# One-hots of the routing table on GpSimd, and the second layer's expert sums kept by token

## The chip, the cores and the metric

The kernel is one program on one core of a Trainium2 chip. The metric is device microseconds of one execution, and lower is better. The kernel before has a median of 5218.21 us over three runs (5210.64 to 5221.29).

## The reference

Two blocks of a model run one after the other on 256 tokens of 1024 channels. The first block has two layers. Each layer mixes tokens and then applies a mixture of 16384 small experts, `peer`; only that part is touched. In layer 0 it runs over 512 tokens (256 of the sequence and 256 of a context), in layer 1 over 256. Cut to what matters:

```python
def block(hc):
    q = (hc @ p['w_q']).reshape(chunk, PEER_HEADS, 2, PEER_HALF)
    s = jnp.einsum('thcd,hcnd->thcn', q, p['sub_keys'])
    s1, i1 = lax.top_k(s[:, :, 0], 16)
    s2, i2 = lax.top_k(s[:, :, 1], 16)
    ...                                   # top 16 of the 256 sums s1 + s2
    gw = jax.nn.softmax(best, axis=-1)
    u = jnp.take(p['peer_u'], eidx, axis=0)          # eidx = i1 * 128 + i2
    act = jax.nn.gelu(jnp.einsum('td,thkd->thk', hc, u)) * gw
    v = jnp.take(p['peer_v'], eidx, axis=0)
    return jnp.einsum('thk,thkd->td', act, v)
```

Each token so picks 128 pairs (i1, i2), 8 heads times 16, each with a weight gw.

## The kernel before, in words

Nothing is gathered. All 128 x 128 experts are computed densely, as 128 blocks e of 128 experts (e is i2's part of the index), and a **routing table** `wd[token, i1, e]` with the weights says what counts. `peer` has three parts.

**Route** (`peer_route`). After the query products, tokens go in blocks b of 128: four in layer 0, two in layer 1. For each block, VectorE finds the top 16 (`topk16`) and makes three arrays of 128 tokens by 128 picks: the two index parts and the weight. TensorE transposes them (`tps`), so that a pick lies on a partition and a token is a column; they land in `tr[0]`, `tr[1]` and `tr[2]`. ScalarE also writes the negatives of the first and the third into `tr[3]` and `tr[4]` (L1099).

**Table** (`peer_table`). For each token two 128x128 matrices are made: `qt`, the one-hot rows of the second index (VectorE, eight tokens in one instruction, L1112), and `pt`, the one-hot rows of the first index times the weight. Of every four tokens two `pt` are made by VectorE in one instruction (L1123), and two by ScalarE in two: the absolute difference from the index (L1120), then the positive part of weight minus weight times that (L1121). TensorE multiplies `pt` and `qt` (`wps`, two instructions for each token in the trace), ScalarE copies four tokens' results out of PSUM (`ws`, L1126), and each 32 tokens are stored by one DMA. A group g is 32 tokens; a block has four.

**Fills.** Expert work that needs no table is put beside the routing: `fill` computes `gelu(u.h)` of an expert block (`gelu_u`: a 512 KB load, a split into high and low parts by ScalarE, L238, and VectorE, L240, 24 products `s` on TensorE, L258, one Gelu) and stashes it in DRAM. 64 of the 128 expert blocks are stashed in each layer. In layer 0 sixteen of them stand behind the last table, in layer 1 four.

**Experts** (`peer_experts`). In groups of four expert blocks, the activations are multiplied with the table's columns, split into `ah` and `al`, the value rows are split into `vh` and `vl`, and `products` forms the three cross terms. In it the value rows are the stationary operand and the activations stream: 24 matmuls for each expert block, 512 columns each in layer 0 and 256 in layer 1. A PSUM tile takes the sum over the four blocks, and `done` (L1226) lets VectorE add it, times a modulation, into `x`. In layer 1 every other group has to compute its `s` first.

The order within an engine's queue is not the order of the code: a scheduler interleaves the instructions of all five engines by its own estimates and by which buffers come free. Each engine then runs its queue strictly in that order. So `s` products and `wps` products are mixed in TensorE's queue in a fixed way, and VectorE's `pt` and `qt` with the next block's top-16 work.

## Time and profile before

| | |
|---|---|
| median of three runs | 5218.21 us |
| the profiled execution | 5211.48 us, its span 5209.7 us |
| TensorE (PE) busy | 4967.9 us, 95% |
| VectorE (DVE) | 3488.0 us, 67% |
| ScalarE (ACT) | 2561.0 us, 49% |
| GpSimd (POOL) | 182.2 us, 3% |
| layer 0, tables of the four blocks | 1290.5 to 1697.3 us |
| layer 1, tables of the two blocks | 3831.7 to 4055.3 us |
| layer 1, experts | 4055.3 to 4626.1 us |

A TensorE matmul's end in the trace is modelled: one of 128 columns stands with 275 ns, while the next can start after less than half of that. So a high busy share hides waits, and the pitch of matmuls in a row (start to start) is what tells how long a piece of work needs. Records of one engine can overlap on VectorE and ScalarE too, by some tens of ns, so there also a pitch is shorter than a duration.

### The profile page before, as it was taken

How to read it: one execution, taken by the hardware profiler on the slowest of the kernel's cores; microseconds unless marked ns; L12 is line 12 of the kernel's file. 1: busy time of each engine (PE TensorE's matmuls, PEld its weight loads, DVE VectorE, ACT ScalarE, POOL GpSimd, SP SyncE). 2: the span in 40 equal slices, each digit the busy share in tenths (PEclk: the TensorE clock that was granted, in tenths of full speed). 3: DMA queues.
4: the chain of work that ended last, by engine and by line, in shares of the span. 5: the costliest groups of instructions: out<-in, count | busy, mean ns of one | idle time of the engine just before them, and what ended most of it. 6: DMA issues, size and time to landing. Idle time of an engine off the chain costs nothing.

```text
span 5209.7 us, 86462 instructions
## 1 busy us (share of the span) xinstructions
PE 4967.9 (95%) x33298; PEld 4170.8 (80%) x33298; DVE 3488.0 (67%) x7830; ACT 2561.0 (49%) x4754; POOL 182.2 (3%) x409
## 2 busy tenths in 40 slices
PE   8999998999999999999999999998899999989989
PEld 6677776678777888888887787877889999987888
DVE  4888878558995455555555566656796777765654
ACT  4345444534989322222223445445478544455564
POOL 0000001000000000000000010101000000000000
PEclk9999999999999999999999899888999999999999
DMA  4332323543444644444442332323656877733544
GB/s 137 107 91 88 90 81 93 167 151 101 160 171 163 234 144 142 142 143 142 143 146 70 111 84 78 85 61 92 210 187 222 279 227 238 226 116 118 167 131 146
DMA packets 432974, 740.50 MB, mean 142 GB/s; under 512 B 132210, under 2 KB 273202, under 8 KB 427826
## 3 DMA queue, kind: packets, MB, share of 16 engines
q1 hardware_dynamic: 431042, 732.29, 44.1%
q8 instruction: 262, 4.29, 0.3%
q10 hardware_dynamic: 1520, 2.69, 0.1%
q14 instruction: 150, 1.23, 0.1%
HBM read 622.37 MB, written 112.49 MB: 141 GB/s over the span
## 4 chain that ended last, share of the span: by engine, by line
PE 74%; ACT 12%; DVE 8%; DMA 3%; issue 2%; SPq 0%; ACTq 0%; POOL 0%; DVEq 0%; POOLq 0%
PE v L1180 20%; PE s L258 14%; PE zps L258 5%; ACT ws L1126 3%; PE adaps L279 3%; PE qps L258 2%; PE ops L258 2%; PE gtps L258 2%; ACT pt L1121 2%; PE ops L1368 2%; ACT whi L238 2%; ACT pt L1120 2%; PE bp L571 1%; DVE wlo L240 1%; PE zbps L258 1%
## 5 line engine op out<-in xcount | busy, mean ns | idle before, releaser
L258 PE MATMUL s<-h,whi 128*128 128x512 f32 (+1 forms) x4096 | 1058.7, 343 | 1.3 <-ACT whi L238 0.7
L240 DVE TENSOR_TENSOR wlo<-wraw,whi 128x1024 fp32r<-128x1024 f32 (+2 forms) x602 | 724.7, 1205 | 470.9 <-ACT whi L238 458.4
L238 ACT CAST whi<-wraw 128x1024 fp32r<-128x1024 f32 (+2 forms) x602 | 621.9, 1034 | 727.0 <-PE s L258 200.0
L258 PEld LDWEIGHTS s<-h,whi 128*128 128x128 f32 x4096 | 703.8, 191 | 68.6 <-ACT ge L1136 1.0
L258 PE MATMUL s<-h,wlo 128*128 128x512 f32 (+1 forms) x2048 | 704.2, 344 | 9.1 <-DVE wlo L240 9.1
L1180 PE MATMUL v<-al,vh 128*128 128x512 f32 (+1 forms) x2048 | 689.7, 337 | 0.6 <-DVE al L953 0.6
L1180 PE MATMUL v<-ah,vl 128*128 128x512 f32 (+1 forms) x2048 | 689.2, 337 | 0.0
L1180 PE MATMUL v<-ah,vh 128*128 128x512 f32 (+1 forms) x2048 | 682.7, 338 | 2.1 <-ACT ah L952 1.5
L952 ACT CAST vh<-vraw 128x1024 fp32r<-128x1024 f32 x256 | 261.9, 1050 | 719.2 <-PE v L1180 574.9
L1226 DVE SCALAR_TENSOR_TENSOR x<-v,mod,x 128x256 f32<-128x256 f32 x768 | 333.7, 477 | 272.6 <-PE v L1180 272.1
L1180 PEld LDWEIGHTS v<-ah,vh 128*128 128x128 f32 x2048 | 387.3, 190 | 49.7 <-ACT ah L952 9.4
L1180 PEld LDWEIGHTS v<-al,vh 128*128 128x128 f32 x2048 | 388.8, 190 | 46.3 <-DVE al L953 4.8
L258 PEld LDWEIGHTS s<-h,wlo 128*128 128x128 f32 x2048 | 390.3, 191 | 44.4 <-DVE wlo L240 10.3
L1180 PEld LDWEIGHTS v<-ah,vl 128*128 128x128 f32 x2048 | 388.1, 190 | 40.3 <-issue 1.4
L953 DVE TENSOR_TENSOR vl<-vraw,vh 128x1024 fp32r<-128x1024 f32 x256 | 308.6, 1220 | 98.9 <-ACT vh L952 98.9
L258 PE MATMUL zps<-h,whi 128*128 128x512 f32 (+3 forms) x896 | 293.6, 407 | 15.5 <-DVE lz L363 7.5
L1125 PEld LDWEIGHTS wps<-qt,pt 128*128 128x128 f32 x1536 | 215.8, 190 | 109.5 <-ACT pt L1121 91.2
L1125 PE MATMUL wps<-qt,pt 128*128 128x128 f32 x1536 | 272.3, 292 | 22.2 <-ACT pt L1121 13.6
L1126 ACT COPY ws<-wps 128x512 f32<-128x512 f32 x192 | 210.5, 1097 | 5.7 <-PE wps L1125 5.2
L258 PEld LDWEIGHTS zps<-h,whi 128*128 128x128 f32 (+1 forms) x896 | 167.5, 198 | 52.8 <-issue 16.6
L279 PE MATMUL adaps<-adaw,cs 128*2 128x128 f32 x1536 | 202.0, 274 | 5.4 <-DMA adaw<-ada 3.2
L1121 ACT ACTIVATE pt<-pt,tr,tr 128x128 f32<-128x128 f32 x384 | 180.4, 489 | 2.5
(614 smaller groups left out, 9617.4 us busy)
## 6 DMA issues: line engine op xcount, KB each, us to landing
wraw<-peu SPq DMA_DIRECT2D x256, 512.0 KB, 4.2
vraw<-pev SPq DMA_DIRECT2D x256, 512.0 KB, 4.5
wraw<-win SPq DMA_DIRECT2D x139, 512.0 KB, 3.6
adaw<-ada SPq DMA_DIRECT2D x96, 512.0 KB, 3.6
wd<-ws SPq DMA_DIRECT2D x24, 2048.0 KB, 6.8
wt<-wd SPq DMA_DIRECT2D x32, 1024.0 KB, 6.8
wraw<-w_q SPq DMA_DIRECT2D x32, 512.0 KB, 3.7
gd<-ge SPq DMA_DIRECT2D x64, 256.0 KB, 2.1
```

The costliest lines, as they stand in the source:

```text
L238: nc.scalar.copy(hi, raw)
L240: nc.vector.tensor_sub(lo, raw, hi.bitcast(F32))
L258: nc.tensor.matmul(out, w[wi][:, k, :], a[ai][:, k, ts], start=n == 0, stop=n == 3 * ko - 1)
L279: nc.tensor.matmul(ps[0:2, i * P:i * P + P], self.cs[:, k, :], w[:, k, :], start=k == 0, stop=k == KO - 1)
L952: self.nc.scalar.copy(hi, src)
L953: self.nc.vector.tensor_sub(lo, src, hi.bitcast(F32))
L1120: nc.scalar.activation(pt, self.iota, AF.Abs, bias=tr[3][:, cs])
L1121: nc.scalar.activation(pt, pt, AF.Relu, bias=tr[2][:, cs], scale=tr[4][:, cs])
L1125: nc.tensor.matmul(ps[:, t, :], pt, qt[:, t1 + t], start=True, stop=True)
L1126: nc.scalar.copy(ws[:, :, t0 + t1:t0 + t1 + 4].rearrange("p i t -> p t i"), ps)
L1180: nc.tensor.matmul(ps[:, m, :], va[i][wi][:, ms], aa[i][ai], start=n == 0, stop=n == 3 * GI - 1)
L1226: nc.vector.scalar_tensor_tensor(x[:, k, ts], src[:, m, ts], self.mod[l][:, 40 + k, s:s + 1], x[:, k, ts], op0=ALU.mult, op1=ALU.add)
```

## The change

Two parts. In the table, the two `pt` of every four tokens that ScalarE made are made by GpSimd, in the same single instruction that VectorE uses; `tr[3]` and `tr[4]` and what writes them go, and `pt` has six buffers in place of four. In layer 1 alone, the products swap operands: the activations of 128 tokens are stationary, and 512 channels of the value rows stream. Four PSUM tiles (two token halves, two channel halves) stay open over all 128 expert blocks. Nothing is added into `x` on the way; at the end `channels` copies the four sums out, transposes them in 16 pieces of 128x128, and calls `done` for each two.

```diff
@@ peer_route
-            tr = [rt.tile([P, T2], F32, name=f"tr{i}") for i in range(5)]
+            tr = [rt.tile([P, T2], F32, name=f"tr{i}") for i in range(3)]
...
                     nc.vector.tensor_copy(tr[n][:, b * P:b * P + P], ps[:, 0:P])
-                    if n != 1:
-                        nc.scalar.activation(tr[3 + n // 2][:, b * P:b * P + P], ps[:, 0:P], AF.Copy, scale=-1.0)
@@ peer_table
-                        pt = wb.tile([P, P], F32, tag="pt", name="pt", bufs=4)
-                        if t % 2:
-                            nc.scalar.activation(pt, self.iota, AF.Abs, bias=tr[3][:, cs])
-                            nc.scalar.activation(pt, pt, AF.Relu, bias=tr[2][:, cs], scale=tr[4][:, cs])
-                        else:
-                            nc.vector.tensor_scalar(pt, self.iota, tr[0][:, cs], tr[2][:, cs], op0=ALU.is_equal,
-                                                    op1=ALU.mult)
+                        pt = wb.tile([P, P], F32, tag="pt", name="pt", bufs=6)
+                        (nc.vector, nc.gpsimd)[t % 2].tensor_scalar(pt, self.iota, tr[0][:, cs], tr[2][:, cs],
+                                                                    op0=ALU.is_equal, op1=ALU.mult)
                         nc.tensor.matmul(ps[:, t, :], pt, qt[:, t1 + t], start=True, stop=True)
@@ peer_experts
+            def products_t(g, va, aa):
+                for i in range(GI):
+                    for b in range(2):
+                        bs = slice(b * P, b * P + P)
+                        for n, (wi, ai) in enumerate(((0, 0), (1, 0), (0, 1))):
+                            for c in range(2):
+                                nc.tensor.matmul(acc[b][c], aa[i][ai][:, bs], va[i][wi][:, c * 512:c * 512 + 512],
+                                                 start=g + i + n == 0, stop=g == P // GI - 1 and i == GI - 1 and n == 2)
+            def channels():
+                rows = []
+                for b in range(2):
+                    r = ep.tile([P, D], F32, tag="vraw", name="vrow", bufs=3)
+                    for c in range(2):
+                        (nc.scalar.copy, nc.vector.tensor_copy)[c](r[:, c * 512:c * 512 + 512], acc[b][c])
+                    rows.append(r)
+                for m0 in range(0, KO, 2):
+                    ps = ps_s.tile([P, 2, T], F32, tag="s", name="vt")
+                    for m in range(2):
+                        for b in range(2):
+                            nc.tensor.transpose(ps[:, m, b * P:b * P + P], rows[b][:, (m0 + m) * P:(m0 + m) * P + P],
+                                                self.ident)
+                    done(m0, ps, True)
+            if T == TX:
+                acc = [[ps_v.tile([P, 512], F32, tag="v", name="acc") for c in range(2)] for b in range(2)]
+                products = products_t
...
+            if T == TX:
+                channels()
```

The change also moves instructions. TensorE's queue in the second group of layer 0's first block, before (`s` is the fills' product, `wps` the table's):

```order
L1125 MATMUL wps<-qt,pt 128x128
L258 MATMUL s<-h_9713,whi 128x512
L258 MATMUL s<-h_9714,whi 128x512
L1125 MATMUL wps<-qt,pt 128x128 x2
L258 MATMUL s<-h_9713,wlo 128x512
L258 MATMUL s<-h_9713,whi 128x512
L1125 MATMUL wps<-qt,pt 128x128
L258 MATMUL s<-h_9714,whi 128x512
L1125 MATMUL wps<-qt,pt 128x128 x3
L258 MATMUL s<-h_9713,wlo 128x512
L258 MATMUL s<-h_9713,whi 128x512
L1125 MATMUL wps<-qt,pt 128x128
```

The same place now:

```order
L1119 MATMUL wps<-qt,pt 128x128 x10
L258 MATMUL s<-h_9713,whi 128x512
L258 MATMUL s<-h_9714,whi 128x512
L1119 MATMUL wps<-qt,pt 128x128 x6
L258 MATMUL s<-h_9713,wlo 128x512
L258 MATMUL s<-h_9713,whi 128x512
L1119 MATMUL wps<-qt,pt 128x128 x6
L258 MATMUL s<-h_9714,whi 128x512
L258 MATMUL s<-h_9713,wlo 128x512
L1119 MATMUL wps<-qt,pt 128x128 x10
L258 MATMUL s<-h_9713,whi 128x512
L258 MATMUL s<-h_9714,whi 128x512
```

The table's products stand close together, and of the fills' 24 products for an expert block two at a time stand between them; the rest follow behind the group. Counted over the whole queue, this is how many `s` products stand between the first table product of a group and that of the next, or, after a last group, up to the next block's table (up to the last table product, where no block follows):

| | before, groups 0, 1, 2, 3 | now |
|---|---|---|
| layer 0, block 0 | 44, 48, 58, 115 | 11, 38, 24, 192 |
| layer 0, block 1 | 40, 49, 48, 151 | 24, 48, 24, 192 |
| layer 0, block 2 | 42, 55, 64, 127 | 24, 48, 24, 192 |
| layer 0, block 3 | 41, 48, 49, 50 | 24, 48, 24, 6 |
| layer 1, block 0 | 102, 106, 116, 376 | 53, 143, 72, 432 |
| layer 1, block 1 | 92, 124, 101, 96 | 72, 144, 72, 10 |

VectorE's queue at the same group before (`qt` and `pt` are the table's, `best`, `pos`, `cand` and `tm` belong to the next block's top 16):

```order
L1112 TENSOR_TENSOR qt<-iota,tr_9788 128x1024
L1123 TENSOR_SCALAR pt<-iota,tr_9787,tr_9789 128x128 x2
L1013 MAX best<-tm 128x8
L1010 MAX best<-cand 128x8
L1014 MAX_INDEX pos<-best,tm 128x8
L1123 TENSOR_SCALAR pt<-iota,tr_9787,tr_9789 128x128 x2
L1112 TENSOR_TENSOR qt<-iota,tr_9788 128x1024
L1011 MAX_INDEX pos<-best,cand 128x8
L1123 TENSOR_SCALAR pt<-iota,tr_9787,tr_9789 128x128
L1012 MATCH_REPLACE tm<-best,cand 128x256
L1057 TENSOR_TENSOR cand<-v_11629 128x256
L1013 MAX best<-tm 128x8
```

And now:

```order
L1110 TENSOR_TENSOR qt<-iota,tr_9788 128x1024
L1117 TENSOR_SCALAR pt<-iota,tr_9787,tr_9789 128x128 x3
L1110 TENSOR_TENSOR qt<-iota,tr_9788 128x1024
L1117 TENSOR_SCALAR pt<-iota,tr_9787,tr_9789 128x128 x3
L1014 MAX_INDEX x_11562<-v_11561,tm 128x8
L1117 TENSOR_SCALAR pt<-iota,tr_9787,tr_9789 128x128
L1110 TENSOR_TENSOR qt<-iota,tr_9788 128x1024
L1117 TENSOR_SCALAR pt<-iota,tr_9787,tr_9789 128x128 x4
L1110 TENSOR_TENSOR qt<-iota,tr_9788 128x1024
L1117 TENSOR_SCALAR pt<-iota,tr_9787,tr_9789 128x128 x3
L1057 TENSOR_TENSOR cand<-v_11561 128x256
L1117 TENSOR_SCALAR pt<-iota,tr_9787,tr_9789 128x128 x2
```

The next block's top-16 work has moved out of the table's groups, most of it behind the fourth; VectorE's `pt` and `qt` follow each other nearly without a break. Counted in the same way, the first three groups hold 17, 53 and 36 instructions of top-16 work in layer 0's blocks 0, 1 and 2 (before 50, 76 and 36), and 27 in layer 1's block 0 (before 50).

TensorE's queue at the end of layer 1's experts, before (`v` is a product, `nps` the norm's sum, `pps` and `gps` belong to the next block of the model):

```order
L1180 MATMUL v<-ah,vh 128x256
L1180 MATMUL v<-al,vh 128x256
L1180 MATMUL v<-ah,vl 128x256
L324 MATMUL nps<-nsq,onesd 128x256 x4
L258 MATMUL pps<-hh_44421,whi 128x256 x2
L258 MATMUL gps<-hh_44421,whi 128x256
L258 MATMUL pps<-hh_44422,whi 128x256
```

And now (`acc` is the open sum, `vt` a transpose of the copied sum):

```order
L1186 MATMUL acc<-vh,ah 128x512 x2
L1186 MATMUL acc<-vl,ah 128x512 x2
L1186 MATMUL acc<-vh,al 128x512 x2
L1201 MATMUL vt<-ident,vrow 128x128 x12
L324 MATMUL nps<-nsq,onesd 128x256 x12
L1201 MATMUL vt<-ident,vrow 128x128 x4
L324 MATMUL nps<-nsq,onesd 128x256 x4
L258 MATMUL pps<-hh_42139,whi 128x256 x2
L258 MATMUL gps<-hh_42139,whi 128x256
```

Each stationary operand is used for two products in a row, and the norm's sums stand behind all products, no longer between them.

## Rows read from the trace of the kernel before

**Rows 1.** Busy time by routing block; its first line names the columns

```profile
core 0: us, PE busy (x) PEld busy (x) DVE busy (x) ACT busy (x) POOL busy (x), PEclk, DMA share, GB/s
1290.50:1392.60 102.10, 97.98 (x517) 74.19 (x516) 94.24 (x276) 93.36 (x187) 0.00 (x0) 1.00 0.45 165
1392.60:1500.40 107.80, 104.59 (x549) 80.94 (x548) 101.21 (x308) 95.15 (x190) 0.00 (x0) 1.00 0.46 166
1500.40:1597.00 96.60, 93.20 (x495) 70.49 (x494) 77.68 (x174) 91.55 (x184) 0.00 (x0) 1.00 0.41 150
1597.00:1697.30 100.30, 98.38 (x517) 73.86 (x516) 52.36 (x94) 88.15 (x183) 0.00 (x0) 1.00 0.46 168
3831.70:3955.30 123.60, 117.61 (x922) 110.61 (x923) 106.34 (x224) 111.73 (x221) 0.00 (x0) 1.00 0.61 216
3955.30:4055.30 100.00, 95.67 (x730) 87.84 (x729) 61.33 (x100) 97.05 (x200) 0.00 (x0) 1.00 0.58 201
```

**Rows 2.** Tile `pt`: count, ns min/median/max, first and last start

```profile
L1125 PE MATMUL wps<-qt,pt x1536: 270/275/378, 1292.3 to 4054.5; 128*128 128x128 f32 x192
L1120 ACT ACTIVATE pt<-iota,tr x384: 378/393/430, 1290.8 to 4052.2; 128x128 f32<-128x128 f32 x192
L1121 ACT ACTIVATE pt<-pt,tr,tr x384: 470/488/522, 1291.4 to 4053.7; 128x128 f32<-128x128 f32 x192
L1123 DVE TENSOR_SCALAR pt<-iota,tr,tr x384: 324/343/351, 1291.6 to 4051.9; 128x128 f32<-128x128 f32 x192
...
  ACT pt L1121: 104.8, 287
```

**Rows 3.** ScalarE by line, 1290 to 1700 us: busy us, mean ns

```profile
L1126 ACT COPY ws<-wps 128x512 f32<-128x512 f32 x128 | 139.8, 1092 | 5.2 <-PE wps L1125 5.2
```

**Rows 4.** VectorE by line, 1290 to 1700 us

```profile
L1112 DVE TENSOR_TENSOR qt<-iota,tr 128x1024 f32<-128x1024 f32 x64 | 78.0, 1218 | 2.3 <-PE wps L1125 2.1
```

**Rows 5.** GpSimd by line, whole span

```profile
L837 POOL TENSOR_TENSOR csum<-csum,lnc 128x256 f32<-128x256 f32 x7 | 5.2, 750 | 7.4 <-ACT lnc L836 6.7 <-ACT bs L578 0.7
...
masks.py:199 POOL TENSOR_SCALAR_AFFINE_SELECT ident<-ident 128x128 f32<-128x128 f32 x1 | 0.3, 292 | 0.1
```

**Rows 6.** Instructions of line 569, GpSimd copies of 128x128

```profile
L569 POOL COPY krp<-kr x224: 288/293/1266, 101.7 to 3621.8; 128x128 f32<-128x128 f32 x112
```

**Rows 7.** Timeline, three places of VectorE beside GpSimd: start us, us, instruction

```profile
884.30 1.26 POOL L837 TENSOR_TENSOR csum<-csum,lnc 128x512 f32<-128x512 f32 x1 [0.59 <-ACT lnc L836]
884.35 1.75 DVE L827 TENSOR_TENSOR lnc<-lnc,mean 128x512 f32<-128x512 f32 x1
...
3087.72 1.25 DVE L240 TENSOR_TENSOR wlo<-wraw,whi 128x1024 fp32r<-128x1024 f32 x1
3088.05 1.08 POOL L569 COPY krp<-kr 128x128 f32<-128x128 f32 x1 [0.15 <-PE bp L573]
...
4623.59 1.82 POOL L1472 MEMSET qe<- 128x2048 f32 x1
4623.81 1.63 DVE L1291 TENSOR_SCALAR bgh<-pv 128x32 f32<-128x32 f32 x1
```

**Rows 8.** Timeline, VectorE in the fourth table of layer 0

```profile
1643.29 1.22 DVE L1112 TENSOR_TENSOR qt<-iota,tr 128x1024 f32<-128x1024 f32 x1
...
1644.43 0.60 DVE L1123 TENSOR_SCALAR pt<-iota,tr,tr 128x128 f32<-128x128 f32 x2
```

**Rows 9.** Timeline, TensorE, eight table products in a row

```profile
1504.24 1.05 PE L1125 MATMUL wps<-qt,pt 128*128 128x128 f32 x8
```

**Rows 10.** Chain that ended last: start us, us, what

```profile
1856.49 21.76 PE s L258 x96
...
4179.43 23.04 PE v L1180 x192
...
4582.63 11.52 PE s L258 x96
```

**Rows 11.** Timeline, TensorE, the last sums of the norm in layer 1

```profile
4624.06 1.99 PE L324 MATMUL nps<-nsq,onesd 128*128 128x256 f32 x8 [1.08 <-ACT nsq L320]
```

## The prediction, made before the run

> **What bounds the kernel now.** I read the page's busy shares first (TensorE 95%), then the chain of waits, then the touched stages by stretch, then their instructions. The change touches two stages, and their limits differ.
>
> In layer 1's experts the chain is TensorE alone: 192 products take 23.04 us and the 96 `s` products of every other group 11.52 us [rows 10], so 0.120 us each, without a gap. ScalarE and VectorE feed it and are not waited for. What counts there is the pitch of products.
>
> In the tables TensorE looks 93 to 98% busy [rows 1], but that is modelled. A table product stands with 275 ns [rows 2], while eight in a row take 1.05 us [rows 9]: (1.05 - 0.275) / 7 = 0.111 us each. An `s` product of layer 0 takes 21.76 / 96 = 0.227 us [rows 10]. With the counts of `s` products from the queue's order and 256 table products for a block (28.4 us), the work in the six blocks is: layer 0, 265 x 0.227 + 28.4 = 88.5, then 93.7, 93.7 and 71.0 us; layer 1 (0.120), 112.4 and 78.0 us. Against the lengths in [rows 1] TensorE idles 13.6, 14.1, 2.9, 29.3, 11.2 and 22.0 us: 93 us in all, the most that the table's part can give beyond what a changed order hides.
>
> Who holds it up? ScalarE is busy 88 to 97% [rows 1], and its one-hots end most of the table's waits (104.8 us [rows 2]). But VectorE is as busy in layer 0's first two blocks (94.2 of 102.1, 101.2 of 107.8), because the next block's top 16 runs there. Only in the last blocks, 52.4 of 100.3 and 61.3 of 100.0, is ScalarE alone the limit.
>
> **The one-hots.** Removed from ScalarE: 384 x (0.393 + 0.488) = 338 us [rows 2]. For four tokens it keeps one copy of 1.09 us [rows 3] of about 2.85; it is no limit any more. Added on GpSimd: 384 instructions that the trace does not show. They depend on `tr` and on a free `pt` buffer, nothing else stands among them in GpSimd's queue, and behind each waits a table product, and behind that all of TensorE's queue.
>
> Their price, from both sides: at least 0.292 us (affine select, 128x128 [rows 5]; a copy of the size has 0.293 [rows 6]); a two-input add of 256 columns has 0.75 [rows 5], so 0.46 for 128 if I take 0.17 as fixed and halve the rest. I take 0.40, between them, since it reads one tensor and does two operations. Above this nothing in the trace bounds it; that risk is priced below. At 64 in a block even 0.46 is 29 us, so GpSimd by itself is no limit. The sign changes of L1099 go too; VectorE makes the first `qt` at that moment anyhow, so I count nothing for them, nor for the two more `pt` buffers.
>
> GpSimd and VectorE hinder each other, though. A VectorE add of 512 columns that began 0.05 us after a GpSimd add of 1.26 took 1.75 us, while one of 1024 columns takes 1.22 [rows 7, 4]. A GpSimd copy that usually takes 0.293 took 1.08 behind a VectorE subtraction [rows 7, 6]. And a VectorE `TENSOR_SCALAR` of 32 columns, the form that makes `pt`, took 1.63 and ended with GpSimd's memset [rows 7]. So all VectorE work of the table (`pt`, `qt`, the fills' `wlo`) excludes GpSimd's instruction, and the other way round. Only the start of the one that waits overlaps: the copy ended 0.16 us after the subtraction, 0.13 less than its 0.293. So one GpSimd one-hot delays VectorE by 0.40 - 0.13 = 0.27 us at most. I take 0.17, two collisions in three, and 0.125 where much single-input top-16 work lies between, with 0 and 0.46 as ends.
>
> [...]
>
> Now the blocks. VectorE's own pitch is 0.25 us for a `pt` and 1.14 for a `qt` [rows 8], so 64 x 0.25 + 16 x 1.14 = 34.2 us, plus four `wlo` (4.6) = 38.8 in a table of layer 0. A top-16 instruction costs 0.39 ((94.2 - 34.2 - 11.4) / 124). By the new order the first three groups hold 17, 53 and 36 of them: 45.4, 59.5, 52.8 and, in the last block, 38.8 us. With the delays (11, 8, 8, 11) the dense parts are 57, 67.5, 61 and, where TensorE's 102 x 0.227 + 28.4 = 51.5 is the longer, 54. The 192 `s` products behind the fourth group are 43.5 us of TensorE, which VectorE's remaining work (under 44) fits beside. The blocks become 100.5, 111, 104.5 and 54 + 19.5 (86 products that moved behind the table) = 73.5, against 102.1, 107.8, 96.6 and 100.3: -1.6, +3.2, +7.9, -26.8, together **-17 us**. Layer 1, with 12 and 14 `wlo`: 58.4 + 11 = 69.5 and, TensorE's 64.2 being the longer, 66; plus 432 and 115 products at 0.120, 51.8 and 13.8: 121.3 and 79.8 against 123.6 and 100.0: **-22 us**.
>
> **The sums by token.** Columns stay the same, instructions halve: 3072 x 0.120 = 368.6 us become 1536 at layer 0's pitch for 128x512, 0.227 [rows 10] = 348.2: -20.4. At 0.120 for 256 columns and 0.227 for 512 each instruction carries some 0.013 us, and half of those go. VectorE loses 31 x 8 additions, which were hidden. Bounds: 0 if a shared bank or a late operand eats it, -21 at best; I take the row's pitch. The end: before, from 4594.15 (the last `s` piece's end [rows 10]) to 4626.05 (the norm's end [rows 11]) is 31.9 us. Now 96 x 0.227 = 21.8, two copies on each of two engines (1.2, by the 1.09 of [rows 3] for a strided one and less for these), the first transposes and additions (1.2), 16 squares on ScalarE at about 0.4 (6.4) and the last sums (0.5): 31.1. So the end pays itself but not the 1.3 us that its last products saved: **-20 us**.
>
> **The sum.** -17 - 22 - 20 = -59 us. From the profiled execution's 5211.5: 5152; the median of the runs shown is 6.7 above that one, so 5152 to 5159. I say **5156 us**.
>
> **Rivals.**
> *The port decides, slower.* Each one-hot delays VectorE by its whole 0.46 us and no start overlaps. For: the 1.63 us row; all of VectorE's table work contends, and the new order packs it densely. Against: the handovers in the same rows do overlap. The blocks change by +16, +25, +29, -13, +16 and -7, +66 in all; with -20, 5258 us. The point from which it decides: above 0.22 us of delay, where TensorE's work no longer covers the last blocks, the six blocks change by -110 + 384 x the delay, so with the -20 the whole is even at 0.34 us. The same if GpSimd by itself needs 1.1 us from start to start.
> *The port costs nothing.* Then the blocks give -13, -5, 0, -29, -11 and -22, and with -20 the time is 5112 us. For: TensorE's queue has 24 `s` products in each group as slack. Against: rows 7.
> *Only the sums pay.* The new order takes the `s` products from the tables, VectorE is the limit in layer 0's first blocks anyhow, and what the last blocks win the others lose: 5211.5 - 20 = 5191 us.
>
> **Chances.** My forecast (20 to 85 us won) 0.50; free port 0.13; only the sums, or a net within 10 us of nothing, 0.14, of which two fifths count as faster; the port or a slow GpSimd instruction 0.23. About 0.2%, 10 us, is what a measurement can tell from no change. Faster by more 0.69, within 0.09, slower 0.22. The range goes from the free port's 5112 to just short of the first rival's 5258: 5110 to 5250. The likeliest case's own range is 5127 to 5191.
>
> **What would show it.** GpSimd's 384 one-hots at 0.3 to 0.5 us, and VectorE's `pt` above 0.343 and `qt` above 1.22 in the mean, by what they wait. Layer 0's last block at 70 to 78 us and layer 1's at 76 to 84; the first three of layer 0 within 10 us of before. The products at a 0.227 pitch, 33.3 us for two groups instead of 34.56. Wrong would be: a one-hot above 0.6 us, blocks of layer 0 above 120 us, or a pitch of products above 0.235.

## The result: slower by 1.0%, and the profile after

The changed kernel takes 5268.59 us (median of 4 runs, 5256.34 to 5286.2) against 5214.86 for the kernel before on the same chip: a ratio of 1.0104, 95% interval [1.0081, 1.0126]. Forecast were 5156 us, with 5110 to 5250 as the range. Of the profiled executions the changed one took 5256.34 us (span 5254.5), 44.8 more in the span than the one before.

First the stretches, cut at the same places as in [rows 1]; the first line names the columns. Lines 1 to 4 are the routing blocks of layer 0, the fifth the fills that are left behind the fourth, the next two the blocks of layer 1.

```profile
core 0: us, PE busy (x) PEld busy (x) DVE busy (x) ACT busy (x) POOL busy (x), PEclk, DMA share, GB/s
1284.90:1400.60 115.70, 99.05 (x520) 80.89 (x519) 95.91 (x262) 53.74 (x57) 68.98 (x64) 1.00 0.41 147
1400.60:1522.00 121.40, 105.64 (x547) 86.68 (x546) 104.40 (x316) 55.04 (x59) 72.22 (x64) 0.99 0.41 147
1522.00:1646.50 124.50, 107.14 (x542) 88.51 (x541) 85.38 (x186) 54.20 (x58) 74.47 (x64) 0.96 0.40 144
1646.50:1728.00 81.50, 66.96 (x382) 55.00 (x381) 47.94 (x87) 40.36 (x43) 70.94 (x64) 1.00 0.38 136
1728.00:1819.20 91.20, 91.20 (x404) 75.50 (x403) 31.93 (x32) 33.13 (x43) 0.00 (x0) 1.00 0.81 282
...
3863.50:4003.80 140.30, 122.39 (x909) 115.37 (x910) 108.38 (x225) 72.56 (x89) 74.53 (x64) 0.95 0.56 195
4003.80:4102.00 98.20, 82.91 (x625) 76.75 (x624) 59.73 (x97) 52.11 (x64) 72.57 (x64) 0.98 0.49 177
```

TensorE's share falls from 95 to 98% to 82 to 87%: it waits more than before, and that although ScalarE, 88 to 97% busy in [rows 1], is down to about half. GpSimd, which did nothing here, is busy 69 to 75 us in each block with 64 instructions, so 1.08 to 1.16 us for each. Layer 0's tables with the fills behind them take 534.3 us, 55.8 more than the same stretch of before; layer 1's tables 238.5 against 223.6.

What the instructions of the tile `pt` take in the changed kernel (ns min/median/max), and below it who ended the waits (us, times):

```profile
L1117 POOL TENSOR_SCALAR pt<-iota,tr,tr x384: 785/792/4097, 1285.2 to 4100.6; 128x128 f32<-128x128 f32 x192
L1117 DVE TENSOR_SCALAR pt<-iota,tr,tr x384: 326/358/553, 1286.0 to 4099.4; 128x128 f32<-128x128 f32 x192
...
  POOL pt L1117: 224.1, 288
```

An undisturbed one-hot on GpSimd takes 0.785 us; VectorE makes the same tile in 0.34 [rows 2]. The waits that ScalarE's one-hots ended (104.8 us, [rows 2]) are gone, and GpSimd's end 224.1 us instead. Both figures add the waits of TensorE's products and of their weight loads, so one standstill can count twice. The products alone, first before and then now, waited for

```profile
  ACT pt L1121: 13.6, 54
...
  POOL pt L1117: 90.8, 95
```

so 77 us more, while the tables' stretches above grew by 55.8 and 14.9 us, the latter although 13.8 us of products have left it. The chain of waits over the first 35 us of the first table says the same, share by line and its first pieces (start us, us, what):

```profile
by line: POOL pt L1117 83.1%; PE wps L1119 12.1%; DMA gd<-ge 6.6%; PE s L258 1.3%; issue 0.6%
...
1285.19 7.79 POOL pt L1117 x6
1292.98 0.04 issue
1293.03 0.73 PE wps L1119 x4
1293.75 12.11 POOL pt L1117 x11
```

And the timeline there, VectorE, GpSimd and the table products:

```profile
1291.09 1.22 DVE L1110 TENSOR_TENSOR qt<-iota,tr 128x1024 f32<-128x1024 f32 x1
1291.09 8.25 POOL L1117 TENSOR_SCALAR pt<-iota,tr,tr 128x128 f32<-128x128 f32 x7
...
1293.03 1.26 PE L1119 MATMUL wps<-qt,pt 128*128 128x128 f32 x6 [1.15 <-POOL pt L1117]
1293.78 0.47 DVE L1117 TENSOR_SCALAR pt<-iota,tr,tr 128x128 f32<-128x128 f32 x1 [0.73 <-PE wps L1119]
...
1297.85 0.49 PE L1119 MATMUL wps<-qt,pt 128*128 128x128 f32 x2 [0.94 <-POOL pt L1117]
```

`qt` keeps its 1.22 us. GpSimd's seven one-hots run without a gap and still take 8.25 us, 1.18 each. VectorE waits for a buffer that TensorE has not yet freed, TensorE for GpSimd.

The second layer's sums did what was forecast of them. The chain that answers to [rows 10]:

```profile
4158.64 11.51 PE s L258 x96
4170.15 21.79 PE acc L1186 x96
```

96 products of 512 columns take 21.79 us, 0.227 each; two groups take 33.30 instead of 34.56 us. From the last table's end to the end of the norm it is 567.0 us instead of 570.75, with 115 more `s` products (13.8 us) in it: 17.6 us won.

One more difference is not the change's. The mixer of layer 1, which the change does not touch, is 20.8 us shorter; its line in the kernel before, and in the changed one:

```profile
2835.10:3690.00 854.90, 801.24 (x7618) 667.73 (x7619) 547.54 (x1462) 412.69 (x919) 82.42 (x194) 0.88 0.32 93
```

```profile
2885.90:3720.00 834.10, 780.62 (x7607) 652.48 (x7608) 545.26 (x1460) 413.03 (x918) 85.92 (x194) 0.90 0.33 95
```

TensorE was granted 0.90 instead of 0.88 of its clock there; the 10 us with the lowest grant have 0.50 in both kernels. That is chance as far as these traces tell: from the mixer's first product to its last the changed kernel takes 859.8 us at 0.90, and the run with the one-hots alone, which has the same instructions there, 872.2 us at 0.89. The medians, 53.7 us apart, show more of the change's cost than the two profiles do.

### The profile page after: what moved, and what is told of

The parts are those of the page before. It is cut to its first block, busy times and chain, and to the rows that moved or that the text cites. A ratio compares the mean times of both kernels' runs of the same rounds, so it can differ in the third digit from the quotient of the medians.

```text
span 5254.5 us, 82985 instructions
## 1 busy us (share of the span) xinstructions
PE 4938.7 (94%) x31778; PEld 4110.7 (78%) x31778; DVE 3414.6 (65%) x7584; ACT 2331.1 (44%) x3976; POOL 618.7 (12%) x793
## 4 chain that ended last, share of the span: by engine, by line
PE 76%; DVE 9%; POOL 6%; ACT 5%; DMA 2%; issue 2%; SPq 0%; ACTq 0%; DVEq 0%; POOLq 0%
PE s L258 17%; PE v L1174 13%; PE acc L1186 7%; POOL pt L1117 6%; PE zps L258 4%; PE adaps L279 3%; PE qps L258 2%; PE ops L258 2%; PE gtps L258 2%; PE ops L1393 2%; DVE wlo L240 1%; PE yp L557 1%; PE bp L571 1%; PE zbps L258 1%; PE up L580 1%
## 5 line engine op out<-in xcount | busy, mean ns | idle before, releaser
L258 PE MATMUL s<-h,whi 128*128 128x512 f32 (+1 forms) x4096 | 1023.0, 340 | 3.2 <-ACT whi L238 2.6
L1117 POOL TENSOR_SCALAR pt<-iota,tr,tr 128x128 f32<-128x128 f32 x384 | 433.7, 1144 | 751.6 <-DVE tr L1097 371.8
L1174 PE MATMUL v<-ah,vl 128*128 128x512 f32 x1024 | 401.6, 392 | 0.0
L1174 PE MATMUL v<-al,vh 128*128 128x512 f32 x1024 | 400.2, 391 | 0.0
L1174 PE MATMUL v<-ah,vh 128*128 128x512 f32 x1024 | 393.3, 391 | 0.5
L1251 DVE SCALAR_TENSOR_TENSOR x<-v,mod,x 128x256 f32<-128x256 f32 x512 | 220.1, 478 | 209.4 <-PE v L1174 209.4
L1119 PE MATMUL wps<-qt,pt 128*128 128x128 f32 x1536 | 256.1, 298 | 97.5 <-POOL pt L1117 90.8
L1174 PEld LDWEIGHTS v<-ah,vh 128*128 128x128 f32 x1024 | 190.9, 188 | 47.6 <-ACT ah L952 7.3
L1174 PEld LDWEIGHTS v<-al,vh 128*128 128x128 f32 x1024 | 192.3, 188 | 45.3 <-DVE al L953 3.9
L1174 PEld LDWEIGHTS v<-ah,vl 128*128 128x128 f32 x1024 | 192.2, 188 | 40.8 <-issue 1.4
L1117 DVE TENSOR_SCALAR pt<-iota,tr,tr 128x128 f32<-128x128 f32 x384 | 139.8, 387 | 123.9 <-PE wps L1119 120.9
```

What stands on the lines that cost most here:

```text
L258: nc.tensor.matmul(out, w[wi][:, k, :], a[ai][:, k, ts], start=n == 0, stop=n == 3 * ko - 1)
L1117: (nc.vector, nc.gpsimd)[t % 2].tensor_scalar(pt, self.iota, tr[0][:, cs], tr[2][:, cs], op0=ALU.is_equal, op1=ALU.mult)
L1119: nc.tensor.matmul(ps[:, t, :], pt, qt[:, t1 + t], start=True, stop=True)
L1174: nc.tensor.matmul(ps[:, m, :], va[i][wi][:, ms], aa[i][ai], start=n == 0, stop=n == 3 * GI - 1)
L1251: nc.vector.scalar_tensor_tensor(x[:, k, ts], src[:, m, ts], self.mod[l][:, 40 + k, s:s + 1], x[:, k, ts], op0=ALU.mult, op1=ALU.add)
```

## The experiments

Three theories stood at the start. **Rate:** GpSimd's one-hot is simply dearer than the prediction's highest price (0.785 us against 0.46), and TensorE waits for it. **Port**, by the prediction's name for it (the traces show who waits, not a port): what hurts is that VectorE and GpSimd exclude each other, so that VectorE too loses time. **Buffers:** with 6 buffers for `pt`, GpSimd can't run ahead and begins too late. Each experiment's ratio is to the kernel before on its chip. "Dense part" is the time from a block's first `qt` to the end of its last `ws` copy, read from the traces. Moving one-hots to another engine, or giving them more buffers, also lets the scheduler change the order within the queues; where that bears on a reading it is said.

| dense parts, us | L0 1st | 2nd | 3rd | 4th | L1 1st | 2nd |
|---|---|---|---|---|---|---|
| changed kernel | 77.6 | 83.5 | 86.8 | 82.6 | 98.9 | 99.3 |
| a quarter on GpSimd | 68.4 | 74.9 | 66.5 | 70.5 | 94.0 | 89.8 |
| all on VectorE | 55.8 | 61.5 | 55.8 | 55.7 | 73.8 | 74.0 |
| all on VectorE, GpSimd beside for nobody | 57.3 | 63.1 | 57.7 | 57.3 | 76.4 | 75.9 |
| changed, 16 buffers | 75.5 | 77.6 | 82.4 | 78.4 | 91.1 | 91.0 |
| a quarter on GpSimd, 16 buffers | 51.3 | 60.1 | 48.3 | 51.4 | 69.3 | 77.2 |
| changed, cheap operation | 55.8 | 65.3 | 62.3 | 63.8 | 72.1 | 78.7 |

### The sums alone

The routing lines are those of before; of the diff only `products_t` and `channels` stay.

> The second part of the change alone: ScalarE makes half of the one-hots as before, the second layer's expert sums are the new ones. In the trace of the changed kernel the stretch of layer 1's experts is 3.7 us shorter although 115 s products (13.8 us) moved into it, so 17.6 us are won there. Theory 1 (GpSimd's one-hot is twice as dear as predicted and nothing else failed): the sums pay 17 to 20 us, so 5195 to 5199 against 5215, and the blocks of the tables stay as before within 3 us each. Rival (the shorter sums only paid because the s products came later): under 8 us won, 5207 or more.

Measured: 5195.57 us against 5210.31, ratio 0.9965 [0.9949, 0.998]. That is 14.7 us, with 10 to 27 in the interval; in the profiles the final norm's `fr` starts 19.4 us earlier, 2.0 of which were won ahead of the last table, so 17.4 in the experts. The rival (shorter only because work came later) falls: here nothing was moved, and it is as much.

### The one-hots alone

```diff
-            if T == TX:
+            if False:
                 acc = [[ps_v.tile(...)
...
-            if T == TX:
+            if False:
                 channels()
```

> The first part alone: one-hots on VectorE and GpSimd in turn, sums by channels as before. If the two parts add up, this is the changed kernel's 5268.6 plus the 17.6 us of the sums, 5286; with the clock's share in the mixer (20.8 us shorter in the changed kernel's profile, by a higher granted clock) taken as chance, up to 5290. Theory 1 and the port rival agree here. Should it come out under 5260, the two parts hinder each other and the sums carry part of the loss.

Measured: 5298.16 us against 5210.31, ratio 1.016 [1.0138, 1.0182]; 8 us more than the highest figure expected. Its dense parts are those of the changed kernel within 1 us but for layer 1's first (101.3). So the whole loss sits in the one-hots, 72 to 95 us of it, and the sums give a part of it back.

### A quarter on GpSimd

```diff
-(nc.vector, nc.gpsimd)[t % 2].tensor_scalar(pt, ...
+(nc.vector, nc.vector, nc.vector, nc.gpsimd)[t].tensor_scalar(pt, ...
```

> The changed kernel, but GpSimd makes only the fourth of each four one-hots, VectorE the other three. 32 on GpSimd in a block at the 1.08 us from start to start that the changed kernel shows are 35 us, under TensorE's 51 to 64; VectorE's dense part becomes 96 x 0.25 + 16 x 1.14 + 4.6 = 46.8 us plus top 16. Theory 1 (GpSimd's rate is the limit, 64 x 1.08 = 69 us in a block): the limit goes, blocks of layer 0 near 97, 111, 104 and 65 us, layer 1's near 121 and 85: 5170 to 5190. Rival, the port (VectorE is held up by each of GpSimd's instructions): half of the hindrance stays and VectorE has more to do, the blocks stay above 105, 118, 115 and 72: 5215 to 5240.

Measured: 5224.34 us against 5210.31, ratio 1.0022 [1.0007, 1.0038]. The port theory's figure, not the rate's: with half of the work GpSimd still ends 183.8 us of waits. One place in the timeline, which repeats every 3.7 us, shows why:

```profile
1291.67 1.22 DVE L1110 TENSOR_TENSOR qt<-iota,tr 128x1024 f32<-128x1024 f32 x1
1291.69 2.80 POOL L1117 TENSOR_SCALAR pt<-iota,tr,tr 128x128 f32<-128x128 f32 x2 [1.18 <-PE wps L1119]
...
1293.70 0.49 PE L1119 MATMUL wps<-qt,pt 128*128 128x128 f32 x2 [0.99 <-POOL pt L1117]
1294.22 1.09 ACT L1120 COPY ws<-wps 128x512 f32<-128x512 f32 x1 [1.09 <-PE wps L1119]
1294.23 0.35 DVE L1117 TENSOR_SCALAR pt<-iota,tr,tr 128x128 f32<-128x128 f32 x1 [0.31 <-PE wps L1119]
```

GpSimd idles 1.18 us for a buffer, begins when `qt` begins, and two one-hots take 2.80 us; TensorE waits 0.99 for the first. `qt` keeps its 1.22 us. So neither theory as stated: GpSimd had time enough on average, but started at the worst moment.

### All on VectorE

```diff
-(nc.vector, nc.gpsimd)[t % 2].tensor_scalar(pt, ...
+(nc.vector, nc.vector)[t % 2].tensor_scalar(pt, ...
```

> The changed kernel, but VectorE makes all the one-hots and GpSimd none. VectorE's dense part is 128 x 0.25 + 16 x 1.14 + 4.6 = 54.8 us plus top 16 (7 to 21 us) in layer 0, about 66 us in layer 1. Theory 1: VectorE is the limit, a little shorter than GpSimd's 69 us: blocks of layer 0 near 105, 119, 112 and 67, layer 1's near 130 and 92: 5210 to 5230. Rival, the port: with GpSimd silent VectorE also loses the hindrance, pt 0.358 to 0.343 us and no gaps, and the time falls below that of the kernel with a quarter on GpSimd.

Measured: 5160.04 us against 5210.31, ratio 0.9893 [0.9874, 0.9911]. VectorE's dense part was estimated at 54.8 us plus top 16, and layer 0's first measures 55.8. The top 16 does not fit beside it: the new order has moved it out. Between a block's first `qt` and its last one-hot VectorE's work other than `qt`, `pt` and `wlo` takes 0.7, 7.0 and 1.1 us in layer 0's first three blocks, in the changed kernel 12.0, 23.4 and 20.1. The time lies 50 us below the 5210 expected at least. The port theory had foretold the order of this one and the quarter on GpSimd; the next run tells whether for its reason.

### GpSimd's work beside it, waited for by nobody

To the kernel with all one-hots on VectorE this adds, at the start of each block's table:

```diff
+        for n in range(64):
+            cs = slice(b * P + 2 * n + 1, b * P + 2 * n + 2)
+            gh = wb.tile([P, P], F32, tag="gh", name="gh", bufs=2)
+            nc.gpsimd.tensor_scalar(gh, self.iota, tr[0][:, cs], tr[2][:, cs], op0=ALU.is_equal, op1=ALU.mult)
         for g in range(b * 4, b * 4 + 4):
```

> All one-hots that anything uses come from VectorE; GpSimd makes 64 more of them in each block into tiles that nobody reads, so no instruction waits for GpSimd. Theory 1 (GpSimd's rate is what hurts: someone waits for its results): no change against the kernel with all one-hots on VectorE, 5150 to 5170, the tables' dense parts stay at 55.8, 61.5, 55.8, 55.7, 73.8 and 74.0 us. The port theory: each of GpSimd's instructions takes its 0.785 us from VectorE, 64 x 0.785 = 50 us in a block, less what falls on VectorE's idle time: dense parts 90 to 106 us in layer 0 and up to 120 in layer 1, the time 5300 to 5440 though nobody waits for the work added. A third, half of the hindrance: dense parts near 80 us, about 5260.

Measured: 5163.91 us against 5211.13, ratio 0.9923 [0.9895, 0.9952]. The kernel without the added work had 0.9893: 64 one-hots beside VectorE in each block cost the whole kernel 0.3%, within what the intervals leave open. The dense parts grow by 1.5 to 2.6 us, so 0.02 to 0.04 us for each. The two engines in this kernel:

```profile
L1108 POOL TENSOR_SCALAR gh<-iota,tr,tr x384: 782/864/3908, 1294.5 to 4023.4; 128x128 f32<-128x128 f32 x192
...
L1121 DVE TENSOR_SCALAR pt<-iota,tr,tr x768: 322/388/476, 1295.4 to 4012.1; 128x128 f32<-128x128 f32 x192
```

GpSimd's 64 are busy 72.8 us in the first block, so 1.14 each, with nothing in their way but VectorE. The port theory falls: the two do interfere, but it is GpSimd that pays.

### Prices

In front of the kernel before stands a list of instructions; the timed lines, in short:

```diff
+ 274  8 x gpsimd.tensor_scalar(128 columns, is_equal, mult, two numbers per partition)
+ 276  8 x the same, is_equal alone
+ 278  8 x is_equal, mult with fixed numbers      280  8 x add, mult with fixed numbers
+ 282  8 x as 274, 512 columns
+ 287 24 x vector.tensor_tensor(1024 columns, add)    289 16 x gpsimd as 274
+ 293 48 x vector.tensor_scalar(128 columns)          295 16 x gpsimd as 274
```

> The kernel before with a list of instructions in front: GpSimd's one-hot of 128 columns eight times with VectorE idle, the same with one operation, with immediate numbers, with add and multiply, with 512 columns; then 16 of them beside 24 VectorE additions of 1024 columns, and 16 beside 48 VectorE one-hots. After the run in which GpSimd's work lay beside VectorE's without harm the theories are: A, GpSimd alone waits, and only behind two-input VectorE work: 0.79 us alone and beside VectorE's one-hots, near 1.1 + 0.79 from start to start beside the additions, VectorE's pitch unchanged (1.14 and 0.25) in both. B, both wait for each other in any form: VectorE's one-hots at 0.25 + 0.79 for each GpSimd instruction between. For the price itself: if 512 columns take four times 128 the price is by column (3.1 us), if under 1.5 us it is mostly fixed.

The timeline of GpSimd and VectorE (start us, us, instruction); line 276 overlaps the end of the additions and is left out:

```profile
2.75 9.93 POOL L274 TENSOR_SCALAR bo<-bsrc,bsc 128x128 f32<-128x128 f32 x8 [1.44 <-DVE bsc L267]
...
20.08 4.89 POOL L278 TENSOR_SCALAR bo<-bsrc 128x128 f32<-128x128 f32 x8
24.94 2.12 POOL L280 TENSOR_SCALAR bo<-bsrc 128x128 f32<-128x128 f32 x8
27.05 16.44 POOL L282 TENSOR_SCALAR bo<-bsrc,bsc 128x512 f32<-128x512 f32 x8
...
43.95 23.21 POOL L289 TENSOR_SCALAR bo<-bsrc,bsc 128x128 f32<-128x128 f32 x16
...
67.61 15.30 POOL L295 TENSOR_SCALAR bo<-bsrc,bsc 128x128 f32<-128x128 f32 x16
```

```profile
3.73 13.60 DVE L287 TENSOR_TENSOR bv<-bw 128x1024 f32<-128x1024 f32 x10
...
68.00 7.31 DVE L293 TENSOR_SCALAR bv<-bw,bsc 128x128 f32<-128x128 f32 x26
```

Alone a one-hot takes 0.787 us (the last ones of line 295, after VectorE stopped; the first of line 274 has 0.805). 512 columns take 2.05, so (2.05 - 0.787) / 384 = 3.3 ns a column and some 0.37 us besides. Fixed numbers make it 0.61, and an addition in place of the comparison 0.265 from start to start: it is the comparison that is dear. Beside VectorE's one-hots it is 0.83 (eight of line 295), and VectorE's stand at 7.31 / 26 = 0.28 instead of 0.25 [rows 8]. Beside two-input additions without a gap each takes 1.40 (line 274 from the third on), one for each addition, and here VectorE loses too: 1.39 us from start to start instead of 1.14 [rows 8] (the 13.60 us above also hold three additions beside line 276). In the second stretch the additions took turns with VectorE's one-hots, and GpSimd's took 1.50 each. So theory A is right that the form of VectorE's work decides and that GpSimd waits most, though its 1.9 us beside the additions was too much. Its "VectorE's pitch unchanged" fails: a two-input instruction loses 0.25 us, far from the 0.79 of theory B.

### Sixteen buffers

```diff
-name="pt", bufs=6)
+name="pt", bufs=16)
```

> The changed kernel with 16 buffers for one-hots instead of 6, so that GpSimd can run further ahead while TensorE works through a row of s products. Theory 3 (six buffers leave GpSimd idle in those rows): layer 1's dense parts fall from 98.9 and 99.3 to 80 to 85 us, layer 0's from 77 to 87 to 70 or so, the time to 5200 to 5230. Port theory (VectorE and GpSimd take turns: a group of 32 tokens costs 16 x 0.25 + 4 x 1.14 + 1.15 + 16 x 0.785 = 22.3 us, whoever waits): dense parts within 5 us, 5250 to 5270.

Measured: 5233.39 us against 5211.13, ratio 1.0049 [1.0032, 1.0067]; by the ratios 0.55% or 29 us less than the changed kernel. Between the two theories: the dense parts fall by 2 to 8 us, most in layer 1, where the rows of `s` products are longest. Against the kernel before the loss falls from 1.04 to 0.49%, so by about half; the rest stays. GpSimd's 64 one-hots of a block all lie in its dense part: with 6 buffers they are busy 70 to 75 us of it and GpSimd idles 8 to 26 us, with 16 they are busy 72 to 79 us and it idles 4 to 15.

### A quarter on GpSimd, and none, with sixteen buffers

The edit of the quarter above and 16 buffers; and the edit of all on VectorE and 16 buffers.

> VectorE three one-hots of four, GpSimd the fourth, with 16 buffers instead of 6. With 6 buffers the trace shows GpSimd beginning its one-hot at the moment a qt begins, waiting its 1.2 us, and TensorE waiting for that one-hot, 18 us for 32 tokens. Theory 3 (too few buffers let GpSimd begin only then): with 16 the wait is hidden, a group costs VectorE's 24 x 0.27 + 4 x 1.14 + 1.15 = 12.2 us or GpSimd's 8 x 0.79 + 4 x 1.1 = 10.7, dense parts of layer 0 50 to 56 us against 66 to 75, the time 5140 to 5165. Rival (GpSimd at such a rate holds the table up in any case): dense parts above 62, 5185 or more.

> All one-hots on VectorE, 16 buffers. VectorE waited only 5 us for TensorE in these instructions with 6 buffers, so both theories expect no change: 5150 to 5165. It is the yardstick for the quarter on GpSimd with 16 buffers: if that one is 10 us or more faster than this, GpSimd's help pays; if this is the faster, any work on GpSimd costs more than VectorE's own.

Measured: 5128.48 us against 5214.5, ratio 0.9842 [0.9823, 0.9861], for the quarter; 5155.57, ratio 0.9888 [0.9872, 0.9904], for none. The quarter beats both kernels and all others that leave nothing out. It is 12 us under the range that theory 3 gave, and GpSimd's help pays: 27 us against none. With 6 buffers the quarter was at 5224: ten more buffers are worth 1.8% here. They also let the scheduler move work: between the first `qt` and the last one-hot of the six blocks stand 12.2 us less of VectorE's other work than with 6. With all on VectorE it is 11.0 us less, and there the ratio stayed (0.9893 with 6 buffers, 0.9888 with 16), so the order does not explain it. The timeline beside the one above:

```profile
1299.34 10.07 POOL L1117 TENSOR_SCALAR pt<-iota,tr,tr 128x128 f32<-128x128 f32 x7
...
1301.41 1.72 PE L1119 MATMUL wps<-qt,pt 128*128 128x128 f32 x14
1301.99 1.21 DVE L1110 TENSOR_TENSOR qt<-iota,tr 128x1024 f32<-128x1024 f32 x1
...
1303.12 1.77 DVE L1117 TENSOR_SCALAR pt<-iota,tr,tr 128x128 f32<-128x128 f32 x6
```

GpSimd's seven take 10.07 us, 1.44 each, and nobody waits for them: `qt` and six one-hots follow each other on VectorE every 2.73 us. The waits that GpSimd's one-hots end are down from 183.8 to 12.3 us (of TensorE's products alone from 83.4 to 5.3). The first blocks of the two layers:

```profile
1288.40:1378.40 90.00, 88.33 (x514) 76.53 (x513) 89.98 (x237) 50.84 (x57) 45.91 (x32) 1.00 0.51 188
...
3773.00:3885.20 112.20, 110.01 (x912) 108.24 (x913) 112.05 (x256) 70.62 (x90) 51.64 (x32) 1.00 0.69 240
```

In these two VectorE is busy all the time; it is the limit now. Against none on GpSimd the 192 one-hots taken from it pay 27 us, 0.14 each.

### An eighth on ScalarE

New sums, no GpSimd; VectorE seven of eight, 6 buffers.

```diff
+if t1 % 8 == 0 and t == 3:
+    nc.scalar.activation(pt, self.iota, AF.Abs, bias=tr[3][:, cs])
+    nc.scalar.activation(pt, pt, AF.Relu, bias=tr[2][:, cs], scale=tr[4][:, cs])
```

> A candidate: new sums, no GpSimd, VectorE makes seven of eight one-hots and ScalarE, in the two operations of before, the eighth. If VectorE's pitch is the limit of the dense parts without GpSimd (14.5 us for 32 tokens), 16 one-hots fewer in a block are 4 us, up to 24 in all: 5136 to 5150 against 5160 with all on VectorE. Rival: ScalarE's 1.1 us copies of the tables and two more operations in each eight hold VectorE's buffers up, no gain: 5155 to 5175.

Measured: 5179.49 us against 5211.13, ratio 0.9938 [0.9917, 0.9959], 0.45% slower than all on VectorE: worse than either expected. Its dense parts are 58.1 to 80.6 us. TensorE's products wait 36.7 us for ScalarE's one-hots here, while the 96 taken from VectorE are worth 96 x 0.25 = 24 us; whether 16 buffers mend that was not tried.

### The changed kernel with a cheap operation

```diff
-(nc.vector, nc.gpsimd)[t % 2].tensor_scalar(pt, ...
+if t % 2:
+    nc.gpsimd.tensor_scalar(pt, self.iota, 1.0, 0.0, op0=ALU.add, op1=ALU.mult)
+else:
+    nc.vector.tensor_scalar(pt, ...
```

> The changed kernel, 6 buffers and all, but GpSimd fills its half of the tiles with an addition and a multiplication by fixed numbers (add 1, times 0), which took 0.293 us alone against 0.787 for the one-hot; every second token's weights are left out of the tables. This is the price that the prediction had as its lower end. Theory 1 (the price is the failed step, the rest of the sum holds): the tables' dense parts fall from 78 to 87 us to 57 to 67 in layer 0 and from 99 to 66 to 75 in layer 1, the time to 5140 to 5170, where the prediction was. Rival (what is wrong is GpSimd's waiting behind VectorE's qt, or the six buffers, whatever the operation costs): the dense parts stay above 70 and 85, the time above 5200.

Measured: 5134.28 us against 5206.73, ratio 0.986 [0.9835, 0.9886]: 2.4% or 127 us under the changed kernel by the ratios, with the same 6 buffers and the same number of GpSimd instructions. In layer 0's tables the instructions of TensorE and of VectorE stand in the same order as in the changed kernel, record for record, so this comparison changes GpSimd's instruction, its price and its inputs, alone.

```profile
L1118 POOL TENSOR_SCALAR pt<-iota x384: 293/299/2149, 1147.3 to 3983.6; 128x128 f32<-128x128 f32 x192
...
  POOL pt L1118: 31.5, 68
```

```profile
1288.80:1383.60 94.80, 92.05 (x524) 79.14 (x523) 91.31 (x262) 52.47 (x57) 36.20 (x64) 1.00 0.50 181
1383.60:1487.10 103.50, 98.74 (x544) 83.96 (x543) 100.77 (x317) 54.67 (x59) 37.21 (x64) 0.98 0.48 171
1487.10:1585.70 98.60, 96.52 (x542) 81.54 (x541) 81.61 (x187) 53.12 (x59) 32.81 (x64) 1.00 0.51 182
```

At 0.293 us alone, 0.57 in place (36.20 / 64, with the waits behind VectorE), GpSimd ends 31.5 us of waits instead of 224.1 (of the products alone 12.1 instead of 90.8), and the blocks take 94.8, 103.5 and 98.6 us where the prediction had 100.5, 111 and 104.5. The dense parts are as theory 1 has them or shorter, but for layer 1's second, 78.7 us against 75 at most. The rival falls. These tiles also don't wait for `tr`: in each block three of the 64 begin before the first `qt`, which is worth 3 x 1.14 = 3.4 us at most, of the 18 to 27 us that a dense part is shorter.

## Why the prediction was wrong

**The step that failed is the price of the one-hot.** The prediction took 0.40 us, between 0.29 and 0.46, from instructions of the same size that do something else. It is 0.787 alone. The 0.17 us that it took as fixed for its 0.46 was an assumption that no run shows; from the one-hots of 128 and 512 columns some 0.37 us stand besides the columns. The two rows it leaned on were sound and not of the kind: a selection by a pattern, and half of an addition of two tensors. An addition in this instruction does take 0.293; the comparison costs as much again and more. "Above this nothing in the trace bounds it" was said, and the sentence behind it, "even 0.46 is 29 us, so GpSimd by itself is no limit", then used the unbounded end as an upper end. In the changed trace the 201 of the 384 that overlap a `qt` or `wlo` take 1.44 us in the mean, the other 183 take 0.81, so 64 are 73 us in a block: more than the 54 to 67.5 us that the prediction gave layer 0's dense parts, and GpSimd's idle time comes on top. That GpSimd's price is the cause, and not the form of the change, is shown by the run with the cheap operation: the order and the buffers are the same, GpSimd still waits behind `qt`, and it ends below the forecast.

**The delay of VectorE was the wrong way round.** The prediction let each one-hot delay VectorE by 0.17 us, 11 us in a block, from [rows 7]. `qt` stayed at 1.218 us in the median, `pt` went from 0.343 to 0.358; the run with GpSimd's work beside lost 1.5 to 2.6 us in a block. GpSimd waits behind the two-input instruction instead (1.40 us beside the additions), and behind `pt`, which the prediction also had as excluding it, hardly at all: 0.83 us instead of 0.79. In [rows 7] GpSimd's instruction was a two-input addition and a memset when VectorE waited; the one row with a GpSimd instruction that reads one tensor, the copy that took 1.08, had GpSimd waiting, and it was the row that applied.

**Who waits for whom.** In the quarter on GpSimd two one-hots that begin with `qt` take 2.80 us, which is `qt` and two one-hots in turn: 1.22 + 2 x 0.79. The other way round `qt` does not wait behind GpSimd's one-hot: 61 of the changed kernel's 96 `qt` begin inside one, and they take 1.22 us in the median, 1.37 at most.

**The buffers were costed at nothing,** "nor for the two more `pt` buffers". With the dear operation 6 in place of 16 cost 29 us at half of the one-hots and 1.8% at a quarter; with the cheap one 6 were enough to come out below the forecast, and no run gave it more. A one-hot takes 0.8 to 2.05 us in the changed trace, seven of them up to 4.1, and must start that much ahead; in the place shown of the quarter on GpSimd it starts when TensorE frees a buffer whose tile is already due.

**The moved `s` products were right in size:** 19.5 us in layer 0 (71.7 to 91.2 us of fills behind the last table), 115 products in layer 1. So was VectorE's own need, 54.8 us for all the one-hots of a block by the prediction's pitches against 55.8 measured (with two `wlo` where the sum has four). With the cheap operation the six stretches that the prediction had at 100.5, 111, 104.5, 54, 121.3 and 66 us, 557.3 in all, measure 94.8, 103.5, 98.6, 63.9, 113.5 and 78.7, 553.0 in all. That the totals are so near is partly luck: each layer's last block is 9.9 and 12.7 us longer than forecast, the other four 5.7 to 7.8 us shorter, and no run takes the last blocks' part apart. (Their 54 and 66 us stand 2.5 and 1.8 us above the work named for them, 51.5 and 64.2, without a reason given; and TensorE's shares in [rows 1] are 95 to 98%, not 93 to 98, which no term uses.)

**The sums** gave 17.6 us in the profile, 17.4 alone, against 20. The pitch came out exactly (0.227 and 33.30 us); the end, from the last `s` product to the end of the norm, takes 32.8 instead of 31.1 us.

**Of the rivals** "the port decides" gave 5258 us, nearest to the result, and for the wrong reason: VectorE isn't held up (`qt` 1.218 us in the median, `pt` 0.358). Its last clause, "the same if GpSimd by itself needs 1.1 us from start to start", named what happened, but put the point of no gain there. At the 1.08 measured in the first table the kernel lost 54 us. The estimate left out that GpSimd also idles: 83 us of it in 21 waits for a table product that frees a buffer.

What stays open: how much of the loss goes with the clock. TensorE was granted 0.99, 0.96, 0.95 and 0.98 of it in four of the changed kernel's blocks and 1.00 in all blocks of before [rows 1]; its products have gaps there that those of before had not. From 1600 to 1605 us, for one, products are busy 2.97 of 5 us, and from 1605 to 1612 the granted clock is 0.76, with 0.50 from 1607 to 1610; that the gaps bring the lower grant no run shows. If the time goes with the grant, I estimate at most (1 - 0.99) x 121.4 + (1 - 0.96) x 124.5 + (1 - 0.95) x 140.3 + (1 - 0.98) x 98.2 = 15 us, and no run takes it apart from the waits themselves.

## What to carry to other kernels

An operation that the trace doesn't show, on an engine with few rows, has no upper price; before moving hundreds of them to where others wait for each, time one alone, with this operation, these operands and the neighbours it will have. Here the work given to a slower engine needed buffers for its whole latency (0.8 to 2.05 us for most one-hots), not for its rate: the same quarter of the one-hots on GpSimd made the kernel 0.2% slower with 6 buffers and 1.6% faster with 16. And moving work from a busy engine to the one that does it best (VectorE, 0.25 us against two operations of 0.39 and 0.49) can beat sharing it out: 0.9893 of the time of before, where the new sums alone give 0.9965.

## What the runs showed of the hardware

GpSimd's `tensor_scalar` of 128 columns costs 0.787 us for a comparison and a product with numbers per partition, from start to start 0.61 with fixed numbers, and 0.265 for an addition and a product with fixed numbers. Beside VectorE's one-input instruction of the same form it slows by 6% (0.83 us); beside a two-input one of 1024 columns it takes 1.40 to 1.50, while that one takes 0.25 us longer from start to start when such work stands back to back on both (1.39 instead of 1.14). In the tables `qt` kept its 1.22 us in the median.
